# Where the condition around overflow tokens stands in an expert layer: in front of the loop over the experts, or at the third expert's beginning

## The chip, the cores and the metric

The kernel runs on one core of a Trainium2 chip, as one program. The metric is the device time of one execution in microseconds. The core has five engines with a queue of instructions each: TensorE (PE, its weight loads PEld), VectorE (DVE), ScalarE (ACT), GpSimd (POOL) and SyncE (SP), which issues most of the DMA transfers.

## The reference, cut to what matters

The model has two layers over 512 tokens of width 1024. Each has a mixer with four branches, a residual with a layer norm, then a feed-forward part. In the first layer that part is dense; in the second it is a mixture of 8 experts with 2 for each token. The change is in the second layer's experts.

```python
def moe_ffn(x, router_w, router_b, w1, w3, w2):
    logits = (x @ router_w).astype(jnp.float32) + router_b
    top_val, top_idx = lax.top_k(logits, TOP_K)              # TOP_K = 2
    weights = jax.nn.softmax(top_val, axis=-1)
    combine = jnp.sum(jax.nn.one_hot(top_idx, N_EXPERTS, dtype=jnp.float32) * weights[..., None], axis=-2)
    y = jnp.zeros_like(x)
    for e in range(N_EXPERTS):                               # 8 experts, D_FF_EXPERT = 1408
        y = y + combine[..., e:e + 1].astype(x.dtype) * swiglu(x, w1[e], w3[e], w2[e])
    return y
```

Everything is float32. An expert's token count is known only on the device: 1024 choices fall on 8 experts, 128 each on average, with no upper bound but 512.

## The kernel before

**Products in float32.** Each weight block of 128 x 1024 elements (512 KB) comes by one DMA into a raw buffer. ACT casts it to a rounded high part (`whi`, L1164), DVE subtracts to get the low part (`wlo`, L1165), and TensorE makes three products for each block of weights: high by high, high by low, low by high (L1428 to L1430 in `up`, L1513 to L1515 in `down`).

**Slots of an expert.** Each expert has 128 main slots and 32 overflow slots (160 together, `NS`). `count` (L1307 on) works out one integer on the chip, `code`: bit e is set when expert e has more than 128 tokens, and 256 is added for each expert with more than 160. `dispatch` makes the lists of token numbers, `tokens` and `more_tokens` gather the rows of these tokens from DRAM by an indirect DMA on POOL.

**Three treatments.** (1) The 128 main slots of each expert: always, in the loop over the experts in `moe`. (2) The 32 overflow slots: in the same loop, in small conditions on bit e of `code` (`further`, used at L1436 and L1519). (3) Tokens past the 160 slots: `rest`, one big condition on `code > 255`. Its body holds a loop over 8 experts and 3 possible further tiles of 128 tokens with a full expert product each (`rest_tile`). With the inputs here the body is not executed: the condition is evaluated, and the engines jump over its code.

**A value in registers.** `values_load` reads `code` into a register of each of the five engines. The same register (`self.more`) then serves the big condition and all small ones.

**The order of the loop.** For expert e there are three chunks of columns (`up(e, 0)`, `up(e, 1)`, `up(e, 2)`, 512, 512 and 384 columns of both `exp_w1` and `exp_w3`), eight raw loads each, and then `down(e)` with eleven loads. `up(e + 1, 0)` is written before `down(e)`, so that at an expert's beginning its first chunk has been multiplied already, and `turn(st)`, `down_more(e - 1)`, `turn_rows` (next expert's rows) and, for e == 2, `more_tokens(1)` follow.

**Who orders.** The program's order gives priorities. A scheduler places the instructions on each engine's queue from it, and may put a later instruction in front of an earlier one where data and buffers allow. Weight loads, casts and subtractions have a raised priority, routing and dispatch the highest (`hot`). Weight loads are chained: each is issued behind the one before it (`self.links["load"]`). A condition is placed as one unit; instructions inside it don't mix with those outside.

**Buffers.** Raw loads of the loop alternate over 13 buffers by a running number (`self.nraw`): 2 of the pool `wp` (`wraw`), 7 of the pool `rf` (`mwraw`), 4 parts of `ring`. Split buffers alternate over 5 by `self.nsp`: 3 of `wp` (`whi`, `wlo`) and 2 of `rf` (`mwhi`, `mwlo`). With `self.common` set, as inside `rest`, only the buffers of `wp` are used. `preload(5)` writes the first five loads of the first chunk and splits two of them ahead of the condition. PSUM has the tags `mm` (3 banks), `s`, `t`, `o`, `r`, `y` (one each). `rest` uses `mm`, `r` and `y`, the buffers of tags `yr` and `xg`, the second half of `xe`, and `gT[0]`.

Of the kernel before, what the change touches and what calls it, by code (L numbers as in the profile page):

```python
# [25 lines left out]
NE = 8  # L26
# [30 lines left out]
class Net:  # L57
# [1490 lines left out]
    def rest(self, dp):  # L1548

        tc, nc, I, mp = self.tc, self.nc, self.I, self.rf  # L1550
        mm = nc.tensor.matmul
        new = lambda name, shape, dt=F32: mp.tile([P] + shape, dt, name=name)
        nt = NE * NR
        cnt = self.cnt
        code = self.more = nc.values_load(self.code[0:1, 0:1], min_val=0, max_val=2 ** NE * (NE + 1) - 1)
        with tc.If(code > 2 ** NE - 1):
            num = self.num_t

            need = new("need", [NE, NR])
            for j in range(NR):  # L1560
                nc.vector.tensor_scalar(need[:, :, j], cnt, float(-NS - P * j), None, op0=OP.add)
            nc.vector.tensor_scalar(need, need, 0.0, None, op0=OP.max)
            needi = new("needi", [NE, NR], I32)
            nc.vector.tensor_copy(needi, need)
            d_need = dp.tile([1, nt], I32, name="d_need")
            nc.sync.dma_start(d_need, needi[0:1].rearrange("p e j -> p (e j)"))
            tk = self.ps("y")
            for e in range(NE):
                for j in range(NR):
                    oh = mp.tile([P, TB, P], F32, name="ohr", tag="yr", bufs=2)  # L1570
                    nc.vector.scalar_tensor_tensor(oh[:, :, 0:P], num[:, None, 0:P].to_broadcast([P, TB, P]),
                                                   float(1 + NS + P * j),
                                                   self.rank[:, :, e:e + 1].to_broadcast([P, TB, P]), op0=OP.add,
                                                   op1=OP.is_equal)
                    q = e * NR + j
                    for b in range(TB):
                        mm(tk[:, q:q + 1], oh[:, b, 0:P], self.num["t"][:, b:b + 1], start=b == 0, stop=False,
                           skip_group_check=True)
                        mm(tk[:, q:q + 1], oh[:, b, 0:P], self.ones, start=False, stop=b == TB - 1,
                           skip_group_check=True)  # L1580
            tf = new("tf", [nt])
            nc.vector.tensor_scalar(tf, tk[:, 0:nt], -1.0, None, op0=OP.add)
            t0 = new("t0", [nt])
            nc.vector.tensor_scalar(t0, tf, 0.0, None, op0=OP.max)
            ti = new("ti", [nt], I32)
            nc.vector.tensor_copy(ti, t0)
            d_tf = dp.tile([nt, P], F32, name="d_tf")
            d_ti = dp.tile([nt, P], I32, name="d_ti")
            nc.sync.dma_start(d_tf.rearrange("q p -> p q"), tf)
            nc.sync.dma_start(d_ti.rearrange("q p -> p q"), ti)  # L1590
            d_cw = dp.tile([NE, P, TB], F32, name="d_cw")
            cw = new("cwe", [NE, TB])
            nc.vector.tensor_copy(cw, self.weights("_r")[1].rearrange("p b e -> p e b"))
            nc.sync.dma_start(d_cw.rearrange("e p b -> p e b"), cw)
            with tc.For_i(0, NE, 1) as e:
                with tc.For_i(0, NR, 1) as j:
                    q = e * NR + j
                    nd = new("nd", [1], I32)
                    nc.sync.dma_start(nd[0:1], d_need[:, bass.ds(q, 1)])
                    left = nc.values_load(nd[0:1, 0:1], min_val=0, max_val=T)  # L1600
                    with tc.If(left > 0):
                        self.rest_tile(e, q, d_tf, d_ti, d_cw, num)
# [162 lines left out]
    def moe(self, dp):  # L1765

        nc, I, mp = self.nc, self.I, self.rf
        self.xe = self.xp.tile([P, 2, 2, KB, P], F32R, name="xe", tag="xh")
        self.ring = self.yg = self.xp.tile([P, 4, D], F32, name="ring", tag="xl")
        with self.hot():  # L1770
            last = self.count()
            with self.tc.issue_after(last.ins):
                self.first_rows(*range(len(FIRST), TB))
            self.split_xe(self.pf, 0)
        self.new_gT()
        self.links = {}
        self.preload(PRE)
        self.common = True
        self.rest(dp)
        self.common = False  # L1780
        self.nraw = self.nsp = -1
        self.links = {}
        with self.hot():
            self.dispatch(range(0, 4))
            g = self.gather(self.xsrc, self.tok[:, 8:9], "xo", self.ring[:, 3])
            self.rows, self.xo = {}, {}
            self.tokens(1)
        st = self.up(0, 0, lambda: self.more_tokens(0, g))
        for e in range(NE):
            gT = self.gT  # L1790
            self.turn(st)
            if e > 0:
                self.down_more(e - 1, yo)
            if e + 1 < NE:
                self.turn_rows(self.rows[e + 1], (e + 1) % 2)
            if e == 2:
                self.more_tokens(1)
            for c in (1, 2):
                st = self.up(e, c)
                if c == 1:  # L1800
                    self.turn(st)
                    self.tokens(e + 2)
                    if e == 0:
                        self.dispatch(range(4, 8))
                    if e == 1:
                        self.wt, self.cw = self.weights("")
                        self.slots()
                    if e == NE - 1:
                        self.ask_rows(0)
                        g, b = self.ln_consts(1, 1)  # L1810
            last = st
            if e + 1 < NE:
                st = self.up(e + 1, 0)
            self.turn(last)
            if e == NE - 1:
                self.take_rows(0)
                self.ask_rows(1)
                self.last_begin()
            yo = self.down(e, gT)
        self.last(yo, g, b)  # L1820
# [45 lines left out]
```

## Time and profile before

| what | value |
|---|---|
| time, median of 3 runs | 2099.56 us (2098.76 to 2100.62) |
| profiled execution, own time | 2099.76 us |
| its span, first to last instruction | 2098.0 us |
| mean granted TensorE clock | 0.988 |
| TensorE busy | 2005.5 us (96%) |
| VectorE busy | 1365.4 us (65%) |
| ScalarE busy | 916.3 us (44%) |
| register load for the condition (L1555), condition (L1556) | 1555 to 1565 us |
| experts' loop, first product to last | 1566 to 2070 us |

All positions are microseconds from the start of the span. The time of an execution is 1.8 us longer than its span. The granted clock is a share of TensorE's full speed; 0.50 is the lower of its two levels.

### The profile page before, as it was taken

How to read it: one execution, taken by the hardware profiler on the slowest of the kernel's cores; microseconds unless marked ns; L12 is line 12 of the kernel's file. 1: busy time of each engine (PE TensorE's matmuls, PEld its weight loads, DVE VectorE, ACT ScalarE, POOL GpSimd, SP SyncE). 2: the span in 40 equal slices, each digit the busy share in tenths (PEclk: the TensorE clock that was granted, in tenths of full speed). 3: DMA queues.
4: the chain of work that ended last, by engine and by line, in shares of the span. 5: the costliest groups of instructions: out<-in, count | busy, mean ns of one | idle time of the engine just before them, and what ended most of it. 6: DMA issues, size and time to landing. Idle time of an engine off the chain costs nothing. (4 is left out here: it accounts for less than half of the span.)

```text
span 2098.0 us, 31138 instructions
## 1 busy us (share of the span) xinstructions
PE 2005.5 (96%) x11240; PEld 1561.3 (74%) x11240; DVE 1365.4 (65%) x2732; ACT 916.3 (44%) x1561; POOL 155.1 (7%) x211
## 2 busy tenths in 40 slices
PE   8999999999999999999999999999989999999984
PEld 7767778778888888888767678778877766677663
DVE  5776779844563333236676779843668877788778
ACT  3464543333232222113454543332326666677663
POOL 1020200000000000000001200000010000000043
PEclk9999999999999999999999999999999999999997
DMA  5231213243243334333221213223538988898872
GB/s 166 71 78 37 58 51 91 81 126 101 91 151 95 101 94 133 91 100 115 77 57 44 70 36 90 84 64 101 196 112 313 350 296 304 284 351 304 291 284 78
DMA packets 274976, 294.56 MB, mean 140 GB/s; under 512 B 23852, under 2 KB 203416, under 8 KB 274808
## 3 DMA queue, kind: packets, MB, share of 16 engines
q1 hardware_dynamic: 267736, 273.90, 40.3%
q0 software_dynamic: 7072, 18.49, 2.8%
q8 instruction: 97, 1.59, 0.3%
q14 instruction: 71, 0.58, 0.1%
HBM read 276.74 MB, written 15.60 MB: 139 GB/s over the span
## 5 line engine op out<-in xcount | busy, mean ns | idle before, releaser
L99 DVE TENSOR_TENSOR wlo<-wraw,whi 128x1024 fp32r<-128x1024 f32 (+1 forms) x218 | 265.4, 1218 | 361.3 <-ACT whi L98 357.4
L98 ACT CAST whi<-wraw 128x1024 fp32r<-128x1024 f32 (+1 forms) x218 | 228.1, 1047 | 622.1 <-PE ps_mm L112 375.7
L113 PE MATMUL ps_mm<-xh,wlo 128*128 128x512 f32 (+1 forms) x1288 | 492.8, 383 | 3.1 <-DVE wlo L99 3.1
L111 PE MATMUL ps_mm<-xh,whi 128*128 128x512 f32 (+1 forms) x1288 | 494.6, 385 | 0.5 <-ACT whi L98 0.4
L112 PE MATMUL ps_mm<-xl,whi 128*128 128x512 f32 (+1 forms) x1288 | 492.4, 383 | 0.2 <-DVE xl L233 0.2
L113 PEld LDWEIGHTS ps_mm<-xh,wlo 128*128 128x128 f32 x1288 | 243.5, 189 | 49.0 <-DVE wlo L99 3.4
L112 PEld LDWEIGHTS ps_mm<-xl,whi 128*128 128x128 f32 x1288 | 243.5, 189 | 45.4 <-issue 2.1
L111 PEld LDWEIGHTS ps_mm<-xh,whi 128*128 128x128 f32 x1288 | 243.2, 189 | 45.3 <-issue 1.9
L1165 DVE TENSOR_TENSOR wlo<-mwraw,whi 128x1024 fp32r<-128x1024 f32 (+1 forms) x98 | 124.1, 1281 | 18.0 <-ACT whi L1164 16.6
L1164 ACT CAST whi<-mwraw 128x1024 fp32r<-128x1024 f32 (+1 forms) x98 | 95.9, 1006 | 16.4 <-PE ps_t L1515 10.2
L472 ACT COPY bt_pt<-ps_t 128x512 f32<-128x512 f32 (+2 forms) x80 | 41.8, 523 | 87.2 <-PE ps_t L467 86.7
L1165 DVE TENSOR_TENSOR mwlo<-mwraw,mwhi 128x1024 fp32r<-128x1024 f32 (+1 forms) x62 | 71.8, 1174 | 6.6 <-ACT mwhi L1164 6.2
L451 ACT ACTIVATE bt_pt<-ps_s,mx 128x256 f32<-128x256 f32 (+3 forms) x128 | 61.9, 488 | 17.5 <-DVE mx L445 14.2
L260 POOL TENSOR_TENSOR rs<-rs,mhalf 128x1 f32<-128x1 f32 x16 | 13.8, 861 | 721.0 <-DVE rs L259 721.0
L442 DVE TENSOR_REDUCE mx<-ps_s 128x2 f32<-128x512 f32 (+3 forms) x80 | 48.5, 607 | 22.5 <-PE ps_s L406 21.8
L1164 ACT CAST mwhi<-mwraw 128x1024 fp32r<-128x1024 f32 (+1 forms) x62 | 61.0, 999 | 3.1 <-DMA mwraw<-in_exp_w_dram 2.0
L1126 DVE TENSOR_TENSOR bt_pt<-bt_pt,ps_mm 128x512 f32<-128x512 f32 x22 | 15.1, 688 | 69.9 <-PE ps_mm L113 62.5
L622 DVE MAX8 m<-bt_pt 128x8 f32<-128x256 f32 (+2 forms) x96 | 53.7, 560 | 2.6
L467 PE MATMUL ps_t<-ident,bt_pt 128*128 128x128 f32 x272 | 45.1, 281 | 8.5 <-DVE bt_pt L461 5.9
L1165 DVE TENSOR_TENSOR wlo<-ring,whi 128x1024 fp32r<-128x1024 f32 (+1 forms) x45 | 51.4, 1158 | 2.5 <-ACT whi L1164 2.4
L623 DVE MATCH_REPLACE8 bt_pt<-m,bt_pt 128x256 f32<-128x256 f32 (+2 forms) x96 | 52.1, 543 | 0.0
L111 PE MATMUL ps_mm<-bt_o,whi 128*128 128x512 f32 x128 | 50.9, 397 | 0.4 <-ACT bt_o L524 0.4
(710 smaller groups left out, 4116.4 us busy)
## 6 DMA issues: line engine op xcount, KB each, us to landing
mwraw<-in_exp_w_dram SPq DMA_DIRECT2D x124, 512.0 KB
wraw<-in_w_in_dram SPq DMA_DIRECT2D x106, 512.0 KB
wraw<-in_ffn_w_dram SPq DMA_DIRECT2D x66, 512.0 KB
ring<-in_exp_w_dram SPq DMA_DIRECT2D x60, 512.0 KB
wraw<-in_exp_w_dram SPq DMA_DIRECT2D x32, 512.0 KB
mwraw<-in_exp_w_dram SPq DMA_DIRECT2D x36, 384.0 KB
wraw<-in_w_branch_dram SPq DMA_DIRECT2D x20, 512.0 KB
wraw<-in_w_out_dram SPq DMA_DIRECT2D x16, 512.0 KB
```

Source lines behind the costliest of these rows:

```text
L98: nc.scalar.copy(h, src)
L99: (low or nc.vector).tensor_sub(l, src, h.bitcast(F32))
L111: mm(ps, wh, xh, start=start, stop=False)
L112: mm(ps, wh, xl, start=False, stop=False)
L113: mm(ps, wl, xh, start=False, stop=stop)
L442: nc.vector.tensor_reduce(mx[:, 0:nh], s3, op=OP.max, axis=AX.X)
L451: nc.scalar.activation(p3[:, h], s3[:, h], AF.Exp, bias=nm[:, h:h + 1], scale=0.125, accum_out=mx[:, 4 + h:5 + h])
L467: return nc.tensor.transpose(pt[:, i * P:(i + 1) * P], p3[:, h, kb * P:(kb + 1) * P], self.ident)
L622: nc.vector.max(m8, sc[:, :nk])
L623: nc.vector.match_replace(sc[:, :nk], m8, sc[:, :nk], REPL)
L1164: self.chain("hi", lambda: nc.scalar.copy(hi[:, :n], src))
L1165: self.chain("lo", lambda: nc.vector.tensor_sub(lo[:, :n], src, hi[:, :n].bitcast(F32)))
```

## The change

The load of `code` into registers leaves `rest` and is made in `moe`, where the condition stood. The condition with its body is now called in the loop, at the beginning of e == 2, in front of `turn(st)`. The running numbers of the buffers are saved and restored around it, so the loop's alternation goes on as if it were not there, and the chain of loads is cut behind it.

```diff
@@ -1552,8 +1552,7 @@
         nt = NE * NR
         cnt = self.cnt
-        code = self.more = nc.values_load(self.code[0:1, 0:1], min_val=0, max_val=2 ** NE * (NE + 1) - 1)
-        with tc.If(code > 2 ** NE - 1):
+        with tc.If(self.more > 2 ** NE - 1):
             num = self.num_t
@@ -1775,11 +1774,9 @@
         self.new_gT()
         self.links = {}
         self.preload(PRE)
-        self.common = True
-        self.rest(dp)
-        self.common = False
         self.nraw = self.nsp = -1
         self.links = {}
+        self.more = nc.values_load(self.code[0:1, 0:1], min_val=0, max_val=2 ** NE * (NE + 1) - 1)
         with self.hot():
             self.dispatch(range(0, 4))
@@ -1788,6 +1785,13 @@
         st = self.up(0, 0, lambda: self.more_tokens(0, g))
         for e in range(NE):
             gT = self.gT
+            if e == 2:
+                n = self.nraw, self.nsp
+                self.common = True
+                self.rest(dp)
+                self.common = False
+                self.nraw, self.nsp = n
+                self.links = {}
             self.turn(st)
             if e > 0:
                 self.down_more(e - 1, yo)
```

## Rows read from the trace of the kernel before

**Rows 1.** The page's first part: busy time, share of the span and instructions.

```profile
PE 2005.5 (96%) x11240; PEld 1561.3 (74%) x11240; DVE 1365.4 (65%) x2732; ACT 916.3 (44%) x1561; POOL 155.1 (7%) x211
```

**Rows 2.** Windows at the stage's start: length, busy by engine, clock, DMA share, GB/s.

```profile
1555.00:1560.00 5.00, 5.00 (x44) 4.83 (x43) 2.85 (x23) 1.38 (x3) 0.00 (x0) 0.72 0.34 128
1560.00:1565.00 5.00, 0.30 (x8) 0.18 (x5) 0.76 (x3) 0.01 (x1) 0.00 (x0) 0.96 0.03 10
1565.00:1570.00 5.00, 4.69 (x18) 3.67 (x19) 3.25 (x8) 4.99 (x5) 0.00 (x0) 0.50 0.94 313
1570.00:1600.00 30.00, 27.27 (x142) 20.73 (x140) 25.84 (x54) 19.77 (x27) 5.13 (x4) 0.98 0.95 339
```

**Rows 3.** The register load by source: duration ns minimum/median/maximum, first and last start.

```profile
L1555 PEldq TENSOR_LOAD <-code x1: 487/487/487, 1560.6 to 1560.6; - x1
```

**Rows 4.** The big condition by source, and the small ones' branch on TensorE.

```profile
L1556 SPq EVENT_SEMAPHORE  x9: 17/17/17, 1558.9 to 1561.4; - x9
L1556 DVEq EVENT_SEMAPHORE  x2: 21/21/21, 1564.0 to 1564.1; - x2
...
L1556 SPq COMPARE_BRANCH  x1: 50/50/50, 1556.4 to 1556.4; - x1
...
L1556 DVEq COMPARE_BRANCH  x1: 72/72/72, 1560.7 to 1560.7; - x1
L1556 PEldq COMPARE_BRANCH  x1: 3612/3612/3612, 1561.2 to 1561.2; - x1
...
L1436 PEldq COMPARE_BRANCH  x66: 76/194/370, 1575.3 to 2032.3; - x66
```

**Rows 5.** Timeline of TensorE: start, us, instruction, idle before it and its releaser.

```profile
1565.12 0.19 PE L1292 MATMUL ps_o<-num_pb,ohs 128*128 128x3 bf16 x2 [4.82 <-PEq L1556]
...
1565.98 0.79 PE L1428 MATMUL ps_mm<-mwhi,xe 128*128 128x512 f32 x1
...
1571.27 0.49 PE L1428 MATMUL ps_mm<-whi,xe 128*128 128x512 f32 x1
...
1575.17 0.63 PE L1365 MATMUL ps_r<-ident,ring 128*128 128x128 f32 x4 [0.91 <-DMA ring<-xs,tok]
...
1578.23 0.40 PE L1428 MATMUL ps_mm<-mwhi,xe 128*128 128x512 f32 x1
...
1581.03 0.40 PE L1428 MATMUL ps_mm<-whi,xe 128*128 128x512 f32 x1
```

**Rows 6.** Timeline of SP: the issues of weight loads around both places.

```profile
1564.10 1.08 SPq L1394 DMA_DIRECT2D wraw<-in_exp_w_dram  x2
...
1683.23 7.40 SPq L1394 DMA_DIRECT2D ring<-in_exp_w_dram  x4
1691.70 6.00 SPq L1394 DMA_DIRECT2D wraw<-in_exp_w_dram  x2
```

**Rows 7.** Timeline of ACT behind the condition.

```profile
1564.99 1.28 ACT L1164 ACT_TABLE_LOAD   x1 [4.99 <-PEq L1556]
...
1571.51 1.05 ACT L1164 CAST mwhi<-wraw 128x1024 fp32r<-128x1024 f32 x1 [1.34 <-PE ps_mm L1430]
```

**Rows 8.** Timeline of POOL: the gather of the first overflow rows.

```profile
1570.70 1.26 POOL L1329 DMA_INDIRECT ring<-xs,tok  x1 [22.03 <-DMA wraw<-in_exp_w_dram]
```

**Rows 9.** Timeline of TensorE among the second expert's last products.

```profile
1687.13 0.60 PE L1462 MATMUL ps_r<-ident,g 128*128 128x128 f32 x4
1687.49 0.48 PE L1514 MATMUL ps_mm<-wlo,gt 128*128 128x512 f32 x1
...
1707.27 1.07 PE L1541 MATMUL ps_y<-yo,ident 128*64 128x512 f32 x2
```

**Rows 10.** Windows before and behind the third expert's beginning.

```profile
1697.00:1709.30 12.30, 12.30 (x64) 7.08 (x57) 6.24 (x7) 6.75 (x9) 0.00 (x0) 1.00 0.74 246
1709.30:1725.00 15.70, 15.18 (x72) 11.62 (x71) 14.37 (x17) 11.72 (x16) 3.77 (x5) 1.00 0.81 282
```

**Rows 11.** DVE's groups by line, 1709 to 1725 us: count, busy, mean ns.

```profile
L1165 DVE TENSOR_TENSOR wlo<-ring,whi 128x1024 fp32r<-128x1024 f32 x2 | 2.4, 1220 | 0.0
```

## The prediction

> **What bounds the kernel now.** I read the page's head first, then a table of windows over the beginning of the expert stage, then the two moved lines by source, then the timelines of each engine around them, and at last the stretch in which the third expert begins.
>
> The head says that TensorE is busy 96% of the span [rows 1]. The reader is to see that this is a kernel where a hole on TensorE goes straight into the time, unless another engine or the DMA is slower in that stretch. [...] TensorE's timeline has it exactly: 4.82 us idle before L1292, ended by TensorE's own queue at L1556 [rows 5].
>
> By source, the hole is not a wait for the tokens' count. TensorE's register load of L1555 is 487 ns at 1560.6 us [rows 3]; its compare and branch at 1561.2 us then takes 3612 ns [rows 4]. The same instruction takes 72 ns on DVE, but DVE's next semaphore event comes only at 1564.0 us, 3.3 us later [rows 4]. The same kind of branch in the small conditions of the loop (L1436) takes TensorE 370 ns at most [rows 4]. The big jump is what is slow: it passes all instructions of the treatment. [...]
>
> Nothing on the far side of the hole was ready either: SP issues the first weight load of the loop at 1564.10 us [rows 6], ACT loads its table first (1283 ns) and then casts [rows 7]. Twelve matmuls run at the low clock, from 1565.98 to 1571.27 us [rows 5].
>
> **The change part by part.** Removed at the start of the stage:
>
> 1. The jump. TensorE is done with the dispatch matmuls at 1560.30. The register load stays there, its end is 1560.6 + 0.49 = 1561.1 us [rows 3], so about 0.8 of the 4.82 us stay: gain 4.0 (bounds 3.3 and 4.8, the latter if the load hides behind matmuls).
> 2. The clock. The twelve matmuls took 5.29 us; twelve later ones, 1578.23 to 1581.03 us, take 2.80 [rows 5]. Gain 2.5. Before the hole, the clock had fallen once (0.72 as a mean of 1555 to 1560) and was back by 1560 (0.96 as a mean of the next 5 us) [rows 2]; an idle 0.8 us should not bring it down again. Bounds 0 and 2.5.
> 3. The thin supply. From 1570 to 1600 us TensorE is idle for 30.00 - 27.27 = 2.73 us [rows 2]. SP can now load the next weights before 1556 us, and the casts need no table load. Against that, the gather of overflow rows (issued at 1570.70 us, waited for at 1575.17 with 0.91 us idle [rows 5, 8]) starts from token numbers that are not ready 5 us earlier just because TensorE is. They come at earliest 1 us behind the last dispatch matmul, and before it was some 4 us (DVE had splits in between); the gather takes 4.5 us from its issue [rows 5, 8]. So TensorE may wait up to 3 us where it waits 0.9. I take a gain of 0.5 (bounds -2.5 and 1.5).
>
> Start: 4.0 + 2.5 + 0.5 = 7.0 us gained, likely within 4.5 and 8.6.
>
> Added at the third expert's beginning, right behind the second expert's last product, at about 1709 us [rows 10]. There the trace has hardly a hole: TensorE is busy 12.30 of 12.30 us before it and 15.18 of 15.70 behind it [rows 10]. So whatever the condition costs there is a new loss:
>
> 4. The jump again. The block jumped over is the same code, so I take 3.61 us [rows 4], and 3.8 with what lies between it and the next matmul. [...] Bounds: 0.4, from the small conditions' branch, and 4.8, the whole old hole.
> 5. The clock. A hole of some 4 us was followed by the low level the last time; at full work that costs 2.5 (part 2). Part of it falls into waits for weights, so 1.5 (bounds 0 and 2.5).
> 6. The restart. The treatment uses the shared weight buffers, both split buffers of `wp`, the PSUM tags `mm`, `r` and `y`, `gt`, and the buffers of tag `xg`. Everything behind it that wants one of these cannot be put in front of it any more. In the trace of before, the transposes of L1462 and the product of L1541 stood between the second expert's matmuls [rows 9]; they take `r` and `y`, as the next expert's transposes do, and now stand behind the jump. By the alternation of buffers, the first load of the new chunk goes to `mwraw`, four to `ring`, the sixth to `wraw`. SP's list shows these same loads: four to `ring` from 1683.23 and two to `wraw` from 1691.70 us [rows 6]. The first five can still be early; from the sixth on all wait for the condition, where before they were issued from 17 us ahead of that place on. The first split goes to `whi` and waits for TensorE's semaphore, as ACT's first cast did at 1565. Table load 1.28, cast 1.05 [rows 7], subtraction 1.22 [rows 11]: 3.55 us until the first chunk is complete. Meanwhile TensorE has work without weights: four groups of four transposes (L1462, its like for the second output, and two for the next expert's rows), the next matmul starting 0.36 us behind the first of a group, and 1.07 for L1541, 2.5 us together [rows 9]. That leaves 1.1. Behind it, DVE sets the pace: it is already busy 14.37 of 15.70 us there [rows 10] and has no splits in hand. And the gather of the second overflow tile takes a buffer of `xg` and so starts behind the jump too; at the stage's start such a gather cost TensorE 0.91 us [rows 5]. For both I add 1.1: 2.2 (bounds 0 and 6).
>
> The loads themselves I cost at nothing: the five early ones are 5 x 6 matmuls x 0.23 = 7 us of TensorE's work, and the sixth should land within 4 us of the end of the jump. If they are not early, that cover is gone and the price is 3 to 4 us, within the bound of 6.
>
> Third expert: 3.8 + 1.5 + 2.2 = 7.5 us lost, likely within 4 and 12.
>
> Sum against the profiled execution of 2099.76 us (span 2098.0 and 1.8 us around it; the median of the runs is 2099.56): 2099.76 - 7.0 + 7.5 = 2100.3, and 2100.1 against the median. I forecast 2100.2: the hole moves and does not vanish.
>
> **The rivals.** [...]
>
> *Slower: the prefetch breaks.* SP passes its own branch by waiting for what is outstanding: its semaphore events of L1556 run from 1558.9 to 1561.4 us though its branch was at 1556.4 [rows 4], and its next load is issued at 1564.10, behind DVE's event [rows 6]. If the five early loads are not early in the new place, the first cast comes some 3.5 us later and up(2, 1) runs at the pace of DMA and DVE: part 6 becomes 6, the sum 11.3, the time 2099.76 - 7.0 + 11.3 = 2104.1; with the gather of part 6 waited for by TensorE, up to 2107. It decides from a loss of 11.2 us on. For it: DMA and DVE are close to TensorE's need there [rows 10]. Against: loads cross the small conditions freely.
>
> *The start does not gain.* If TensorE now waits for the gather or the register load there, and the clock falls all the same, part 1 to 3 give 2.5: 2105. For it: nothing but the gather's 4.5 us [rows 5, 8]; against: 24 matmuls need no gather.
>
> **How the numbers follow.** A change of 0.2% is 4.2 us, and that is about what a measurement of this kernel can tell from none. Forecast (within 2095.6 and 2104.0): 0.50. Cheap jump, faster: 0.22. Broken prefetch 0.18 and start without gain 0.10, both slower: 0.28. The range reaches into both sides, 2094.0 to 2106.5; the forecast's own is 2096 to 2104.
>
> **What would show it.** Right: no hole over 1.5 us on TensorE between 1559 and 1568 us and a clock of 1.00 there; the third expert's beginning with one TensorE hole of 3.5 to 5 us behind the last matmul of L1515, a branch of about 3.6 us on TensorE, a clock of 0.50 for some us behind it; first weights of up(2, 1) split only after it; up(0, 0) about 7 us earlier. Wrong: a branch of a few hundred ns; holes behind the jump that sum to over 5 us with DMA or DVE as releaser; or a wait for the gather of over 2 us at the start.

## The result, and the profile after

The changed kernel takes 2117.3 us (median of 4 runs, 2115.7 to 2118.3) against 2100.1 (2098.8 to 2101.7): ratio 1.0080, 95% interval 1.0067 to 1.0094, so 14 to 20 us slower. The forecast was 2100.2 with a range up to 2106.5. The profiled execution took 2115.65 us (span 2113.9, clock 0.980). TensorE has as many matmuls as before [rows 1], but is busy 13.5 us longer with them:

```profile
PE 2019.0 (96%) x11240; PEld 1574.1 (74%) x11240; DVE 1367.8 (65%) x2732; ACT 920.5 (44%) x1562; POOL 154.4 (7%) x211
```

**The stage's start.** The 4.82 us hole at the condition [rows 5] is gone, as forecast, but the first product of the experts starts at 1574.22 instead of 1565.98. TensorE's timeline in the changed kernel, with the third expert's place at its end (M marks which experts each token of a block has chosen; there are four blocks):

```profile
1563.35 0.17 PE L1262 MATMUL ps_y<-M,tris 128*128 128x8 bf16 x1 [1.61 <-DVE M L1259]
1564.17 0.24 PE L1311 MATMUL ps_y<-M,ones 128*128 128x8 bf16 x4 [0.65 <-DVE rank L1265]
...
1574.22 0.77 PE L1428 MATMUL ps_mm<-mwhi,xe 128*128 128x512 f32 x1
...
1713.25 0.39 PE L1515 MATMUL ps_mm<-whi,gt 128*128 128x512 f32 x1
1719.67 1.09 PE L1462 MATMUL ps_r<-ident,g 128*128 128x128 f32 x4 [6.04 <-DVEq L1555]
...
1722.09 0.79 PE L1428 MATMUL ps_s<-whi,xe 128*128 128x512 f32 x1 [0.47 <-ACT whi L1164]
```

The routing itself is late: DVE makes the last M (L1259) at 1563.14, before at 1553.12. Why shows on SP's queue (L106 is the last load of the residual's product, L211 the residual's rows, L1171 to L1177 the router's vectors, L216 the stores of finished rows, L1394 the experts' weights). Its timeline before:

```profile
1510.67 4.10 SPq L211 DMA_DIRECT2D bt_x<-xs  x8
...
1519.79 2.49 SPq L1177 DMA_DIRECT2D rgb<-in_ln_b_dram  x1
1529.87 19.17 SPq L216 DMA_DIRECT2D xs<-bt_x  x6
```

and in the changed kernel:

```profile
1511.16 0.37 SPq L106 DMA_DIRECT2D wraw<-in_w_out_dram  x1
1511.57 1.89 SPq L211 DMA_DIRECT2D bt_x<-xs  x4
1516.64 0.38 SPq L1394 DMA_DIRECT2D wraw<-in_exp_w_dram  x1
1517.06 1.90 SPq L211 DMA_DIRECT2D bt_x<-xs  x4
...
1526.81 0.38 SPq L1394 DMA_DIRECT2D wraw<-in_exp_w_dram  x1
1527.23 0.98 SPq L1394 DMA_DIRECT2D mwraw<-in_exp_w_dram  x2
1528.26 0.47 SPq L1177 DMA_DIRECT2D rgb<-in_ln_g_dram  x1
1532.16 1.00 SPq L216 DMA_DIRECT2D xs<-bt_x  x2
1533.22 0.46 SPq L1177 DMA_DIRECT2D rgb<-in_ln_b_dram  x1
1536.99 17.39 SPq L216 DMA_DIRECT2D xs<-bt_x  x4
...
1689.97 7.11 SPq L1394 DMA_DIRECT2D ring<-in_exp_w_dram  x4
1719.66 0.96 SPq L1394 DMA_DIRECT2D wraw<-in_exp_w_dram  x2
```

Without the condition in front of them, four weight loads of the loop are placed between the transfers of the residual and the router. Two of them go to `wraw`, which DVE's last subtractions of the residual still read, and SP's queue stands still in front of them. From the waits of SP, 1495 to 1570 us (in all, times, longest):

```profile
SPq L1394 <- DVE wlo L99: 6.3, 2, 3.2
```

Behind the first stand four of the eight row loads (DVE waits 2.79 us for them); behind the second the router's vectors and row stores that wait in turn for DVE (L274, 21.3 us in five waits). The vector `rgb ln_b` is issued at 1533.22, before at 1519.79; the first logits (L1252) come at 1543.41, before at 1529.77. DVE's timeline, with its work at the third expert's beginning:

```profile
1522.04 0.69 DVE L1053 SCALAR_TENSOR_TENSOR bt_x<-bt_x,ps_o 128x512 f32<-128x512 f32 x1 [2.79 <-DMA bt_x<-xs]
...
1543.41 0.22 DVE L1252 SCALAR_TENSOR_TENSOR lg<-rsum,mv,ps_r 128x8 f32<-128x8 f32 x1
...
1713.67 0.69 DVE L1533 COPY yr<-ps_mm 128x512 f32<-128x512 f32 x1 [8.78 <-PE ps_mm L1515]
1714.78 2.36 DVE L1165 TENSOR_TENSOR mwlo<-ring,mwhi 128x1024 fp32r<-128x1024 f32 x2 [0.41 <-ACT mwhi L1164]
```

While the routing is late, TensorE has mostly small matmuls, is idle for 2.85 us between 1560 and 1570, and the granted clock is low. In the windows it is third from the end. Before:

```profile
1550.00:1560.00 10.00, 7.86 (x69) 7.29 (x67) 7.85 (x55) 1.38 (x3) 0.00 (x0) 0.83 0.52 169
1560.00:1570.00 10.00, 4.99 (x26) 3.86 (x24) 4.01 (x10) 5.00 (x5) 0.00 (x0) 0.73 0.49 161
1570.00:1580.00 10.00, 8.79 (x38) 6.57 (x37) 9.74 (x36) 4.49 (x6) 3.17 (x3) 0.93 0.78 259
```

The same stretches in the changed kernel, and two of the third expert's beginning, which had 1.00 in both before:

```profile
1550.00:1560.00 10.00, 9.64 (x48) 9.35 (x48) 6.02 (x28) 0.46 (x1) 0.92 (x1) 0.52 0.32 107
1560.00:1570.00 10.00, 7.15 (x44) 6.07 (x42) 6.21 (x33) 0.00 (x0) 0.00 (x0) 0.65 0.29 105
1570.00:1580.00 10.00, 10.00 (x50) 8.18 (x50) 5.41 (x21) 2.22 (x3) 2.91 (x3) 0.50 0.17 39
1700.00:1720.00 20.00, 13.96 (x71) 8.34 (x71) 7.47 (x8) 6.31 (x8) 1.55 (x2) 0.92 0.17 63
1720.00:1740.00 20.00, 18.78 (x77) 13.66 (x75) 14.83 (x19) 15.59 (x22) 3.42 (x4) 0.83 1.01 369
```

**The third expert.** TensorE stands 6.04 us, where before it was idle for 0.5 us in a longer stretch [rows 10]. Its own branch takes 3.71 us and is passed at 1717.5; DVE's event at 1719.5 ends the hole. By source:

```profile
L1555 PEldq EVENT_SEMAPHORE  x2: 51/51/51, 1717.6 to 1717.7; - x2
L1555 DVEq EVENT_SEMAPHORE  x2: 21/21/21, 1719.5 to 1719.6; - x2
...
L1555 PEldq COMPARE_BRANCH  x1: 3710/3710/3710, 1713.8 to 1713.8; - x1
...
L1555 DVEq COMPARE_BRANCH  x1: 63/63/63, 1715.7 to 1715.7; - x1
```

DVE comes later than TensorE: a copy and two subtractions stand in front of its branch, which fill the first 3.5 us of the hole (to 1717.1), and its event follows 2.4 us behind them. Behind the hole ACT loads its table again (1.28 us, as in [rows 7]), and TensorE works at the low clock (0.50 from 1720 to 1726). The two parts can be followed on ACT's copy of each expert's result (L1532), the milestone that the experiments use: it lies 5.3 us later than before for the first expert, 13.5 for the third and 15.7 for the seventh.

### The profile page after: what moved, and what is told of

The parts are those of the page before. It is cut to its first block, busy times and chain, and to the rows that moved or that the text cites. A ratio compares the mean times of both kernels' runs of the same rounds, so it can differ in the third digit from the quotient of the medians.

```text
span 2113.9 us, 31139 instructions
## 1 busy us (share of the span) xinstructions
PE 2019.0 (96%) x11240; PEld 1574.1 (74%) x11240; DVE 1367.8 (65%) x2732; ACT 920.5 (44%) x1562; POOL 154.4 (7%) x211
## 5 line engine op out<-in xcount | busy, mean ns | idle before, releaser
L260 POOL TENSOR_TENSOR rs<-rs,mhalf 128x1 f32<-128x1 f32 x16 | 13.9, 870 | 728.6 <-DVE rs L259 717.0
```

## The experiments

Times against the kernel before run on the same chip; the difference is (ratio - 1) x 2100 us.

| run | median us | ratio, 95% interval | difference us |
|---|---|---|---|
| changed kernel | 2117.3 | 1.0080 (1.0067 to 1.0094) | +16.8 |
| e1 no condition | 2110.3 | 1.0051 (1.0037 to 1.0064) | +10.7 |
| e2 loads held | 2104.6 | 1.0026 (1.0014 to 1.0038) | +5.5 |
| e3 both places | 2110.2 | 1.0057 (1.0044 to 1.0071) | +12.0 |
| e4 small body | 2110.0 | 1.0056 (1.0043 to 1.0070) | +11.8 |
| e5 held, no condition | 2097.9 | 0.9987 (0.9977 to 0.9997) | -2.7 |
| e6 held, small body | 2102.7 | 1.0013 (1.0004 to 1.0022) | +2.7 |
| e7 held, one copy | 2095.7 | 0.9976 (0.9967 to 0.9985) | -5.0 |
| e8 held, last expert | 2104.2 | 1.0018 (1.0009 to 1.0027) | +3.8 |
| e9 early, free buffers | 2113.2 | 1.0066 (1.0054 to 1.0078) | +13.9 |
| e10 held, first expert | 2109.1 | 1.0048 (1.0035 to 1.0061) | +10.1 |
| e11 held, half body | 2100.3 | 1.0010 (1.0001 to 1.0019) | +2.1 |
| e12 behind router vectors | 2105.9 | 1.0026 (1.0017 to 1.0035) | +5.5 |
| e13 the same, no condition | 2098.0 | 0.9991 (0.9982 to 1.0000) | -1.9 |

Positions in the profiled runs scatter by up to 3 us already at L106 of SP's queue, an instruction ahead of everything that differs (1510.26 before, 1510.2 to 1513.3 elsewhere). Where a position is said to be counted from L106, this scatter is taken out of it; the others stand as the traces have them.

### e1: no condition

```diff
-            if e == 2:
-                ...
-                self.rest(dp)
-                ...
```

> The changed kernel without the big condition at all: the treatment of tokens past the 160 slots is left out (its body is not executed with these inputs). The register load stays in front of the loop. Theory A (the loss at the start of the expert stage comes from what the condition in front of the loop had kept in order, and the third expert costs about 9 us by itself): 2117.3 - 9 to 12 = 2105 to 2108, so still slower than the kernel before (2100) although no condition is left. Rival (the start gained its 7 us as the prediction said and all of the loss is at the third expert): 2093.

Measured: +10.7 us. No big condition is left, and the kernel is still slower than before: the first part of the loss is at the start. The condition's removal is worth 16.8 - 10.7 = 6.1, less than the 9 to 12 that were expected.

### e2: the loop's loads behind the last row store

```diff
 def store_x(self, tb, dst):
-            self.nc.sync.dma_start(dst[...], self.x[tb][h])
+            self.stored = self.nc.sync.dma_start(dst[...], self.x[tb][h])
 def moe(self, dp):
         self.nraw = self.nsp = -1
-        self.links = {}
+        self.links = {"load": self.stored}
```

> The changed kernel with one edit: the chain of the loop's weight loads begins behind the store of the last residual row, so that SP's queue issues the residual's and the router's transfers in the order of the kernel before, and the loop's weight loads behind them. Condition at the third expert as in the changed kernel. Theory A (the early weight loads, each waiting for its buffer on SP's queue, hold up the transfers of residual and router vectors and so the routing): the first logits (L1252) come back from 1543.4 to about 1530 us, the first expert product (L1428) from 1574.2 to 1560 to 1567, time 2099 to 2107. Rival (the loss comes from the register load, the early casts or another order on TensorE, not from the loads): first logits at 1543, time 2115 to 2119.

Measured: +5.5; the first logits are back at 1531.69, the first product at 1564.97. Theory A's numbers. ACT's early casts are still early here (1537.92, 1543.39, 1546.87), so they were not the cause. At the third expert the hole is again 6.04 us.

### e3: the condition in both places

```diff
+            if e == 2:
+                ...
+                self.rest(dp)
+                ...
             self.turn(st)
```

> The kernel before, with its condition in front of the loop kept, and the same condition once more at the third expert's beginning. The start should be as in the kernel before; what is added is the cost of the third expert's place alone. By the prediction's parts 4 to 6: 2100 + 7.5 = 2107.6. By the milestones of the two traces (the copy of the result at L1532 falls back by 9.3 us from the second expert to the third, and by 2.5 between the fourth and the fifth): 2100 + 9.3 to 11.8 = 2109 to 2112. Rival (the third expert's place costs all 17 us): 2117.

Measured: +12.0 (9.2 to 14.9), at the upper end of the milestones' estimate. The line that loads `code` into registers is inside `rest`, so e3 runs it twice as well. Its first expert's copy, counted from L106, is 3.1 us earlier than in the profile of before, with the same program up to there: so much does the start scatter from execution to execution.

### e4: a small body at the third expert

```diff
         with self.tc.If(self.more > 2 ** NE - 1):
-            (whole treatment)
+            for i in range(3): raw load, split, mm3x, copy to yr, turn_main
+            self.turn_rows(self.gather(self.xsrc, self.tok[:, 0:1], "xg"), 1)
```

> The changed kernel with a small body in the condition at the third expert: three raw loads with their splits and products, one addition, one gather, in the buffers that the treatment uses; the treatment itself is left out. The order around the condition stays about the same, and only what has to be jumped over shrinks. Theory A (the hole is the jump past a large block): TensorE's branch under 0.4 us instead of 3.71, its hole there 0 to 2 instead of 6.04 us, the clock stays at 1.00, time 2117.3 - 5 to 8 = 2109 to 2112. Rival (the cost is in the shared buffers and the order, not in the jump): hole 4 us or more, 2115 to 2118.

Measured: +11.8, and the branch 0.21 us. The time is theory A's, the hole is not: 3.71 us, again ended by DVE, which passes its branch only behind the copy and the two subtractions. So the jump is not the whole price. As its start happened to be faster (first expert's copy 2.40 us later than before, against 5.27 in the changed kernel), the two times do not size the jump; e6 does.

### e5: e2 without the condition

```diff
 (as e2)
-            if e == 2: ... self.rest(dp) ...
```

> e2_loads_held without the condition at the third expert: the treatment of tokens past the 160 slots is left out. What is left of the change is its start alone, with the loads in the order of the kernel before: the case that the prediction's parts 1 to 3 describe. If they are right: 7.0 us under the kernel before (2098.9), 2092; the milestones of e2 give 4.6 to 6.5 us, 2092.4 to 2094.3. Theory A (two separate causes, loads at the start and the condition at the third expert): e2 (2104.6) minus the third expert's 8 to 9.5, 2095 to 2096.6 by the medians. Rival (the early loads do not matter, e2 gained by another way): no gain on the kernel before, 2099 or more.

Measured: -2.7 (-4.8 to -0.6): a gain, but well short of 7.0; the 2097.9 us are above theory A's 2095 to 2096.6 too. e2 less e5 is 8.2 for the third expert, and e1 less e5 is 13.4 for the place of the loads. With e5's own -2.7 the two causes make 18.9, against 16.8 in the changed kernel: they add up, within their intervals of 2 to 3 us each.

### e6 and e7: what of the third expert's price is the jump

```diff
 (as e2, and in e6 the body of e4; in e7:)
         with self.tc.If(self.more > 2 ** NE - 1):
+            self.nc.vector.tensor_copy(t, self.y[:, 512:520])
```

> e2_loads_held with the small body of e4 in the condition at the third expert (treatment left out). It parts the third expert's cost into the jump past a large block and the place in the order. By e4's milestones (4.8 us of 7.6 to 8.9 are left with a small body): the time of e5 + 4 to 5.5 = 2097 to 2100, and a TensorE hole of 3.7 us ended by DVE, which has a copy and two subtractions in front of its branch. If the jump is all: the time of e5 + 0 to 1.5.

> e2_loads_held with a body of one DVE copy that reads the second expert's result rows and shares no buffer with what comes behind (treatment left out). The branch is still in the same stretch. If the rest of e6's cost is the sharing (TensorE's transposes wait until DVE has passed the condition, loads and splits wait behind it): no TensorE hole over 0.6 us there and the time of e5 + 0 to 1.5. If a condition costs by itself wherever five engines pass it: a hole of 3 us or more and the time of e6.

Measured: e6 +2.7, 5.4 over e5; e7 -5.0, no dearer than no condition at all. By source and waiters, e6:

```profile
L1550 PEldq COMPARE_BRANCH  x1: 208/208/208, 1702.1 to 1702.1; - x1
...
L1550 DVEq COMPARE_BRANCH  x1: 63/63/63, 1704.0 to 1704.0; - x1
L1550 DVEq EVENT_SEMAPHORE  x1: 21/21/21, 1705.5 to 1705.5; - x1
...
  PE ps_r L1462: 3.7, 1
```

and e7, where TensorE's timeline shows no idle time in the stretch:

```profile
L1552 PEldq COMPARE_BRANCH  x1: 226/226/226, 1703.9 to 1703.9; - x1
```

The reader is to see that the branch itself costs 0.2 us in both. What e6 pays is that TensorE's transposes (L1462) take a PSUM buffer that the body uses too: they have to wait until DVE has passed the body, and DVE has other work first. One more effect is in e6 and not in e7: with buffers shared, SP issued no weight load from 1686 us on until DVE had passed. The jump is the rest, 8.2 - 5.4 = 2.8 us, with an uncertainty of some 3. The milestones put the two nearer to each other: from the first to the seventh expert's copy, e6 is 4.9 us longer than e5, and e2 4.4 longer than e6.

### e8 and e10: other places

```diff
-            if e == 2:
+            if e == NE - 1:        (e8; body in the other half of xe)
+            if e == 0:             (e10)
```

> e2_loads_held with the whole condition at the last expert's beginning in place of the third's (the body takes the other half of the row buffer, which is free there). In the trace of before TensorE is idle some 11 of 20 us at 2040 to 2060, behind DVE and GpSimd, so that a hole at about 2010 may be taken up there. If it is taken up in part: 2096 to 2101. If each condition costs its 8 to 9 us wherever it stands: the time of e2, 2104.

> e2_loads_held with the whole condition at the first expert's beginning in the loop, behind up(0, 0), in place of the third's. There TensorE is idle 2.7 of 30 us anyway and less is in hand. If the price is that of the jump and the restart wherever TensorE has work: 7 to 9 us over e5 (2098) = 2105 to 2107. If the thin supply there hides part of it: 2100 to 2104.

Measured: over e5, the last expert costs 6.5 and the first 12.8. At the last nothing was taken up, and the estimate for the first was exceeded. In e10 TensorE's branch took 5.57 us and a second hole of 3.43 followed. In e8 the hole at the jump nearly vanished, though the branch took 3.94 us: TensorE's sequencer reached it at 1998.5, while matmuls handed over earlier ran on until 2003.3. Its timeline:

```profile
2002.94 0.39 PE L1515 MATMUL ps_mm<-whi,gt 128*128 128x512 f32 x1
2004.26 0.63 PE L1462 MATMUL ps_r<-ident,g 128*128 128x128 f32 x4 [0.93 <-DVEq L1555]
...
2007.95 1.86 PE L1541 MATMUL ps_y<-yo,ident 128*64 128x512 f32 x2 [2.62 <-DVE sgo L1484]
```

The price came back in the stretch behind it (TensorE busy 6.39 of 10 us from 2000 on at a clock of 0.90, and 0.75 in the next ten, where e5 has 9.79 and 1.00 twice). Of all places measured with the whole body, the one in front of the loop is the cheapest: it costs what e13, e5 and e7 gain, 2 to 5 us.

### e9: loads early, but into free buffers

```diff
-        self.nraw = self.nsp = -1
+        self.nraw, self.nsp = 1, -1
```

> The changed kernel with the running number of the raw buffers begun two further on, so that the loop's first loads go to buffers that are free instead of two that the residual's last subtractions still read. Two loads (1 MB) are still issued in front of the residual's, but SP does not wait in front of them; the next stand behind the row stores. Theory A, as a wait in SP's queue (6.3 us of waiting for DVE's subtractions in front of the loads, and the residual and router transfers behind them): the first logits come back from 1543.4 to 1530 to 1534 us, and the time falls to that of e2, 2102 to 2107. Rival (the loads hurt as traffic, wherever they go): first logits still 3 us or more late (1536 to 1543), time 2108 to 2117.

Measured: first logits at 1533.52, as theory A said, but +13.9 in time. DVE still waits 2.8 us and TensorE 2.0 for the residual's rows, behind 1 MB of weights. The edit also shifts the rotation of buffers in the whole loop, so its time does not tell wait from traffic: inconclusive, and the reason for e12. Its trace says a little more. Counted from L106, the last M comes at 45.3 us, against 42.9 before and 52.0 in the changed kernel: with loads in front that need not wait, 2.4 of the 9.1 us are left. The first expert's copy is still late (135.1 us from L106; 137.7 in the changed kernel, 127.3 in e2), and the third expert costs as much as elsewhere (from the first to the seventh expert's copy 9.6 us more than in e5).

### e11: half the body

```diff
-            with tc.For_i(0, NE, 1) as e: ... self.rest_tile(...)
+            self.turn_rows(self.gather(self.xsrc, self.tok[:, 0:1], "xg"), 1)
```

> e2_loads_held with only the first part of the treatment in the condition (need, the 24 lists of tokens by 192 products, the weights), without the loops over the further tiles (left out). It asks whether the price of the jump grows with the code that is passed. TensorE's branch was 0.21 us past the small body and 3.3 to 3.9 us past the whole one. If it is in proportion to the code: 1.5 to 2.5 us. If it is one fetch as soon as the code behind is not at hand: 3.3 to 3.9 us again, and the time of e2, 2104.

Measured: the branch takes 4.73 us, not less than with the whole body; the price does not go by the amount of code. Time +2.1, 4.8 over e5, less than the expected 2104 us. In the trace the sequencer is 1.9 us ahead of the last matmul's end, and DVE has passed before TensorE (its event is at 1708.1). By source and TensorE's timeline:

```profile
L1555 PEldq COMPARE_BRANCH  x1: 4730/4730/4730, 1707.0 to 1707.0; - x1
```

```profile
1712.06 0.63 PE L1462 MATMUL ps_r<-ident,g 128*128 128x128 f32 x4 [3.21 <-PEq L1555]
```

The hole is 3.21 us and no clock loss follows (1.00 from 1700 to 1730 us), where the 6.04 us hole, and one of 3.70 in e6, were followed by the low level.

The trace has one more thing on the long branches. DMA queue 8 brings instructions in packets of 16 KB, 97 in the kernel before, one in some 22 us. Inside the changed kernel's branch (1713.8 to 1717.5 us):

```profile
q8 instruction: 1, 0.02, 2.2%
```

All ten long branches of the traces have exactly one such packet inside them, and end 1.4 us behind its end; the three short ones (e4, e6, e7) have none. In most the packet starts 1.0 us behind the branch's start; in e11 it starts 2.4 us behind it. That the branch waits for this packet is read from this regularity; no run tests it.

### e12 and e13: the same loads, another place on SP's queue

```diff
 def route_begin(self):
-            nc.sync.dma_start(gb[:, i], I[n][1, 0]...)
+            self.stored = nc.sync.dma_start(gb[:, i], I[n][1, 0]...)
 def moe(self, dp):
-        self.links = {}
+        self.links = {"load": self.stored}
 (e13: and no condition, as e1)
```

> The changed kernel with the chain of the loop's weight loads begun behind the router's last small load (rgb ln_b, L1177) in place of the last row store (e2): the same four loads with the same buffers are issued early, about 25 us ahead of e2, as traffic beside the row stores and the routing, but nothing that the residual or the router needs stands behind them on SP's queue except the row stores. Theory A (the place in SP's queue, in front of the residual's rows and the router's vectors): first logits at 1530 to 1533 us, first product at 1564 to 1567, time that of e2 or below, 2100 to 2106. Rival (2 MB of traffic during the routing is what costs): first logits or the last M (L1259, 1553 before, 1563 in the changed kernel) 3 us or more late, time 2108 to 2117.

> e12 without the condition at the third expert (treatment left out). With e12 it gives the third expert's price once more, in a pair that differs in nothing else: 8 us (e2 less e5 gave 0.39% of 2100 = 8.2; the prediction's term is 7.5). Against the kernel before it gives the start's gain: 7 by the prediction, 2.5 by e5's median, 4.3 by e5's milestones at the third to seventh expert. If the early loads bring something more than in e5: 2092 to 2096; if not: 2096 to 2098.

Measured: e12 +5.5, e13 -1.9. SP's timeline in e12:

```profile
1511.12 4.14 SPq L211 DMA_DIRECT2D bt_x<-xs  x8
...
1521.08 2.30 SPq L1177 DMA_DIRECT2D rgb<-in_ln_b_dram  x1
1523.49 1.16 SPq L1394 DMA_DIRECT2D wraw<-in_exp_w_dram  x2
1524.70 0.97 SPq L1394 DMA_DIRECT2D mwraw<-in_exp_w_dram  x2
1530.53 18.61 SPq L216 DMA_DIRECT2D xs<-bt_x  x6
```

The same four loads into the same buffers are issued within 7 us of where the changed kernel has them, and the loss at the start is gone: the last M is at 1553.55 instead of 1563.14. The changed kernel less e12 is 11.3 us, e1 less e13 12.6. So it is the place in the queue, in front of the residual's rows and the router's vectors, and not the early loading. e12 less e13 gives the third expert once more: 7.4.

## Why the prediction was wrong

**The step that failed is part 3**, with the whole of "Start: 7.0 us gained". Part 3 is a gain of 0.5 (bounds -2.5 and 1.5): it says "SP can now load the next weights before 1556 us" and books that as help. The loads did come 38 to 47 us earlier, but no term asked what stands behind them on SP's queue and what they wait for. Shown by e2 and e12: that place costs 11 to 13 us, and it is not in any rival. The nearest, "The start does not gain", names a wait of TensorE for the gather or the register load; neither ended a wait here.

**Parts 1 and 2 were too large as well.** In the kernels with the order restored and no price at the third expert, the start gives 2 to 5 us (e13 -1.9, e5 -2.7, e7 -5.0) and not 7.0. Two reasons can be read. First, the hole of 4.82 goes, but not all of it is gained. From the counting matmul (L1311) to the first product TensorE has the same 65 matmuls in all these kernels. Before, that took 12.14 us, with 5.01 idle; in e5 it takes 9.08. There the 65 come in another order and are busy 8.26 us instead of 7.13, at about the same mean clock (0.81 and 0.80), and 0.82 us are idle for comparisons of DVE (L1290), which stand on its queue behind a wait of 2.77 us for ACT (L1353). So part 1 gave from 0.6 (e12, with a clock of 0.50 in this stretch) to 3.2 (e13), below its bound of 3.3. Second, the clock of part 2 is not tied to the hole alone: it is low during the routing in some executions without the hole, and high there in one with it (e3, 1.00 from 1550 to 1565 us). Windows of 1550 to 1560 and 1560 to 1570 us, first of e12, then of e5:

```profile
1550.00:1560.00 10.00, 7.50 (x47) 6.66 (x46) 8.05 (x39) 0.00 (x0) 0.00 (x0) 0.68 0.52 170
1560.00:1570.00 10.00, 9.21 (x49) 7.53 (x49) 5.50 (x21) 2.05 (x3) 1.69 (x2) 0.50 0.04 5
```

```profile
1550.00:1560.00 10.00, 7.50 (x60) 6.89 (x59) 9.71 (x46) 0.29 (x1) 0.92 (x1) 0.86 0.64 201
1560.00:1570.00 10.00, 9.18 (x64) 7.56 (x65) 6.83 (x23) 3.27 (x4) 2.16 (x2) 0.97 0.67 229
```

From L106 to the first expert's copy, the eight profiled kernels with the order restored and no condition at the first expert take 126.5 to 130.1 us (e5 the shortest, e12 the longest), the two with the old start 133.4 (before) and 130.3 (e3). The means are 3.9 us apart. About 1 us of that is given back behind the seventh expert's copy: from there to the end of the span e5 takes 88.8 us and the kernel before 87.7.

**Parts 4 to 6 held as a sum, not in its terms.** Forecast 7.5 us, likely within 4 and 12; measured 8.2 (e2 less e5), 7.4 (e12 less e13), 6.1 (changed kernel less e1) and 12.0 (e3, with its second register load). The milestones agree better than the times: from the first to the seventh expert's copy, the condition adds 9.3, 9.0, 8.9 and 9.1 us in these four pairs, of which 0.6 to 1.6 are made up by the end of the span. That the sum came out so near is in part luck.

Part 4 is right in the branch (3.71, forecast 3.6), but the hole is 6.04, not 3.8, since DVE and not TensorE passes last; the prediction had read DVE's 3.3 us in the front place and not asked what DVE has queued in the new one. Part 5 is right in kind: the clock is at 0.50 behind the hole. Part 6: the sharing that it names is about half of the price (5.4 by the times and 4.9 by the milestones with a small body, e6), the jump the other half (2.8 and 4.4). The gather of part 6 did not matter: L1365 waits 0.30 us, for a small condition. The prediction put the slow jump down to the instructions that it passes; half the code cost no less (4.73 us in e11, 3.34 with the whole in e2), and each long branch has one 16 KB packet of instructions inside it. What makes the branch long is not shown beyond that.

Of the outcomes with a chance of their own, "Cheap jump, faster" (0.22) fell (branches of 3.3 to 5.6 us past half or all of the code in every place tried; only in e8 did one lie under matmuls, and the price stayed). "Prefetch breaks" was partly true: SP issued four loads to `ring` and then none for 22 us up to 1719.66, but the third expert's price stayed within the bounds. Of what the prediction would have taken as a sign of being wrong, nothing came: no short branch, no holes of 5 us behind the jump's own, no wait for the gather. None of its signs looked at SP's queue at the start.

Open: what delays the packet of instructions at the first expert (2.7 us behind the branch's start and 1.6 long, in a branch of 5.57 us; elsewhere with the same body 1.0 to 1.6 behind and 0.9 to 1.4 long, in branches of 3.3 to 3.9); why DVE's event comes 2.4 us behind its last work at the third expert and at once in e8; and whether e9's wait for the residual's rows is traffic alone. No place was found in which the whole condition makes a kernel faster than the one before; the versions that beat it (e5, e7, e13) leave the treatment out.

## What to carry to other kernels

Here the condition that all engines pass also kept the scheduler's order: without it in front of the loop, four weight loads came ahead of the router's last vectors and the row stores, and SP stood 6.3 us in front of two of them. Before moving such a condition, list what may now slide ahead on each queue, which buffer each of these waits for, and what small transfer stands behind; then hold it behind that transfer with an explicit order, as in e12 (11.3 us less than the changed kernel). At the new place, price the engine that passes last, with the work queued in front of its branch (DVE here, with a hole of 6.04 us beside a TensorE branch of 3.71), and the buffers that the body shares with what follows (5.4 us in e6): a condition with a small body that shares none cost nothing here (e7).

## What the runs showed of the hardware that was not expected

- TensorE's compare and branch took 0.21 to 0.23 us past a small body and 3.3 to 5.6 us past half or all of the treatment; half the code (4.73 us) was not cheaper than the whole (3.34 in e2). Each of the long ones has one 16 KB packet of instructions inside it.
- A long branch can lie under matmuls: 3.94 us of branch with a hole of 0.93 us (e8), where the sequencer reached it 4.8 us ahead of the last matmul's end.
- DVE's own branch is recorded with 56 to 72 ns, but the event behind it came 3.8 us later at the third expert of the changed kernel (2.4 us behind the end of DVE's last work) and 0.7 us later in e8 (2003.4 to 2004.1, as soon as that work ended).
- Two waits of 3.2 us and less in front of weight loads on SP's queue went with first logits 13.6 us later, about twice their sum: a 4 KB vector stood behind them and then behind row stores. With the same loads behind that vector they came at 1530.42 (e12; 1529.77 before).
